# Value products of two heads in one 128-column matmul, with a new order of patterns and query loads

## The chip, the core and the metric

The kernel runs on one core of a Trainium2 chip. The metric is the device time of one execution in microseconds (us). The core has a matrix engine (PE, with its weight loads listed as PEld), a vector engine (DVE), a scalar engine (ACT), a general engine (POOL) and a queue (SP) that issues all DMA transfers of this kernel in the order of the program. Each engine runs its own instructions in program order and waits for the others through semaphores.

## What is computed

One layer of a hybrid decoder: 4096 prompt positions and 32 sample positions go through one input projection. Half of the result feeds attention with 8 heads of 64, half a gated recurrence; both are gated, joined, projected back and normalised. The part that the change touches is the prompt's attention. Each head looks back along the sequence in three patterns, (window, stride) = (128, 1), (512, 4) and (2048, 16), with 128 keys each:

```
def _dilated_prompt(q, k, v, d):
    """Dilation d: split positions into d stride classes (keys gathered by stride) and run
    the window attention inside each class."""
def _band_attention(q, k, v):
    s = jnp.einsum('nbqhd,nbkhd->nbhqk', qb, kc) * (dh ** -0.5)
    p = jnp.exp(s - m[..., None])
    o = jnp.einsum('nbhqk,nbkhd->nbqhd', p, vc) / den...
def _merge(parts):
    ws = [den * jnp.exp(m - m_max) for (_, m, den) in parts]
    return sum(w[..., None] * o for w, (o, _, _) in zip(ws, parts)) / total[..., None]
```

All values are float32.

## The kernel before, in words

Four phases follow one another. Phase 1 projects q, k and v. Phase 2 is the attention, with the matmuls of the attention's gate woven in as filler. Phase 3 is the recurrence, phase 4 the output projection, the normalisation and the sample's attention. The change lies in phase 2 (line 405), which takes the time from 592 to about 1490 us of the profiled execution.

Phase 2 works through 8 units. A unit is a pair of heads and one half of the sequence (2048 positions, in four spans of 512). The keys of the pair lie in the tile `KT` (`S1` or `S_77` in the traces), its queries in `QT` (`S0`, `S_76`), one quarter of which belongs to each span `nb`. A unit has 48 steps. A step is 128 queries of one pattern for both heads. In the code the pattern `pat` is 0 for stride 16, 1 for stride 4 and 2 for stride 1. The order of a unit's steps is written out in the list `order` (line 738): four steps of stride 4 and four of stride 1 on span 0, then 16 steps of stride 16 (`a` = 0 to 3, over all spans), then four of stride 4 and four of stride 1 on each of the spans 1 to 3. A span is complete with the fourth step (`b` = 3) of its last pattern; span 0 with the last step of stride 16.

Step `i` is spread over the loop of line 772, which counts steps in `now`:

- `gather_q` (line 457), three steps ahead: POOL copies the step's queries in stride order into `qg`. Stride 1 needs no gather; PE reads `QT` itself.
- `front` (line 510), at step `i`: PE writes the scores of both heads into `s` (lines 515 and 516, two matmuls a head), DVE adds the mask and takes the minimum (line 522), ACT takes the exponential (line 526) into `sm`.
- `feed`: about four filler matmuls (lines 653 to 658, 256 columns each).
- `middle` (line 529), two steps later: PE transposes `sm` into `pt` (line 535), DVE or ACT copies it to `pts` (lines 539 and 541); the list `ev` says which.
- `back` (line 543), four steps later: PE multiplies `pts` by the values into `o` (line 551).

In most steps the band has two blocks of 128 keys (`x.full`); at the start of the sequence it has one. I call them full and half steps. All patterns' first steps of a sequence are half steps: 21 of the 48 steps in the units with the first half of the sequence (units 0, 2, 4 and 7), none in the others. That is 300 full and 84 half steps.

`back` before the change: for each block of keys and each head one matmul with the 64 value columns of the head as stationary operand and 128 moving columns; head 0 writes partitions 0 to 63 of `o`, head 1 partitions 64 to 127. Four steps fill a bank of `o`; after the fourth, ACT copies the whole bank to `u` in SBUF.

Merging the three patterns runs along behind, by calls that `defer` puts a number of steps after the end of a span: `stats_out` (3 steps), `stats_in` (6), `weights` (11), `weights_b` (12), `spread` (15, the DMA `gb<-wd` that brings the weights back, spread over partitions), `combine` (17 to 20, five POOL instructions on the tile `gb`, the first in line 620, the others recorded in line 798) and `store` (21). `load_Q` (line 396, four DMAs of 256 KB) fetches the next unit's queries of a span two steps after the span's end. POOL runs gathers and combines in one order, SP runs all DMAs in one order.

Of the kernel before, what the change touches and what calls it, by code (L numbers as in the profile page):

```python
# [8 lines left out]
F32 = mybir.dt.float32  # L9
# [14 lines left out]
SPAN = 512  # L24
# [6 lines left out]
class Kern:  # L31
# [373 lines left out]
    def phase2(self):  # L405
# [136 lines left out]

        def back(x):
            kbs = (0, 1) if x.full else (1,)
            if x.b == 0:
                x.grp.o = ps_o.tile([128, 512], F32, tag="o", name="o")
            o = x.grp.o
            for kb in kbs:
                v = v_ap(x.c, x.st, x.pat, x.a, x.b, kb)
                for h in range(2):  # L550
                    nc.tensor.matmul(o[h * 64:(h + 1) * 64, x.b * 128:(x.b + 1) * 128],  # L551
                                     v[:, h * 64:(h + 1) * 64], x.pt[:, h, kb],
                                     start=(kb == kbs[0]), stop=(kb == 1), skip_group_check=True)
            if x.b == 3:
                if x.pat == 0:
                    nc.scalar.copy(x.unit.u16.rearrange("p (i r) -> p r i", r=16)[:, 4 * x.a:4 * x.a + 4],
                                   o.rearrange("p (r i) -> p r i", r=4))
                else:
                    t = up.tile([128, SPAN], F32, tag=f"u{x.pat}", name="u", bufs=4 - x.pat)
                    if x.pat == 1:  # L560
                        nc.scalar.copy(t.rearrange("p (m r) -> p r m", r=4), o.rearrange("p (r m) -> p r m", r=4))
                    else:
                        nc.scalar.copy(t, o)
                    x.unit.u[x.pat, x.a] = t


        def stats_out(un, nb):
# [43 lines left out]
        def combine(un, nb):  # L611
            s, gb = slice(nb * SPAN, (nb + 1) * SPAN), un.gb[nb]
            e = nc.gpsimd
            for k, (f, o, y) in enumerate(((e.tensor_mul, 0, un.u16[:, s]), (e.tensor_mul, 1, un.u[1, nb]),
                                           (e.tensor_mul, 2, un.u[2, nb]), (e.tensor_add, 0, gb[:, 1]),
                                           (e.tensor_add, 0, gb[:, 2]))):
                if k:
                    defer(min(k, 3), f, gb[:, o], gb[:, o], y)
                else:
                    f(gb[:, o], gb[:, o], y)  # L620
# [114 lines left out]
            units.append(un)  # L735
        steps = []
        for un in units:
            order = [(1, 0), (2, 0)] + [(0, w) for w in range(4)]
            for nb in range(1, 4):
                order += [(1, nb), (2, nb)]  # L740
            for pat, a in order:
                grp = S()
                for b in range(4):
                    x = S()
                    x.unit, x.c, x.st, x.pat, x.a, x.b, x.grp = un, un.c, un.st0, pat, a, b, grp
                    steps.append(x)
# [18 lines left out]

        vload(0)
        vload(4)
        for x in steps[:3]:
            gather_q(x)
        feed(self.f0[0])  # L770
        N, staged, split = len(steps), 0, 0
        for i in range(N + 26):
            now[0] = i
            if i < N:
                x = steps[i]
                un = x.unit
                if x.pat == 1 and x.a == 0 and x.b == 0:
                    un.u16 = u16p.tile([128, ST], F32, tag="u16", name="u16")
                    un.ac = sp.tile([128, 3, 16, 2, 2], F32, tag="ac", name="ac")
                    if un.i < 6 and un.st0 == 0:  # L780
                        defer(self.kl[0], load_K, un.c, 4, 2)
                        defer(self.kl[1], load_K, un.c, 6, 2)
                if x.pat and x.b == 0:
                    un.st[x.pat, x.a] = sp.tile([128, 4, 2, 2], F32, tag=f"st{x.pat}", name="st")
                x.stat = un.ac[:, 0, 4 * x.a + x.b] if x.pat == 0 else un.st[x.pat, x.a][:, x.b]
                front(x)
# [3 lines left out]
            if 0 <= i - 2 < N:  # L790
                middle(steps[i - 2])
            if i + 3 < N and steps[i + 3].pat < 2:
                gather_q(steps[i + 3])
            for k in (1, 5):
                if i + k < N and (steps[i + k].pat == 0) == (k == 1):
                    vload(i + k)
# [5 lines left out]
            if i >= self.wl[1] and credit[0] < -10 ** 8:  # L802
                for _ in range(self.wl[2]):
                    if split < staged:
                        wx_split(split)
                        split += 1
            if i < N and x.b == 3 and (x.pat == 2 and x.a or x.pat == 0 and x.a == 3):
                nb = x.a if x.pat else 0
                for d, f in zip(self.lag, (stats_out, stats_in, weights, weights_b, spread, combine)):
                    defer(d, f, un, nb)  # L810
# [1 line left out]
                if un.i + 1 < 8:  # L812
                    v = units[un.i + 1]
                    if nb == self.kl[4] and un.i % 2 and un.i < 6:
                        defer(self.kl[5], load_K, v.c, 0, 2)
                        defer(self.kl[6], load_K, v.c, 2, 2)
                    if nb and un.i == 5:
                        if nb < 3:
                            defer(self.kl[2], load_K, v.c, 3 + nb, 1)
                        else:  # L820
                            defer(self.kl[3], load_K, v.c, 6, 2)
                    defer(2, load_Q, v.c, v.st0, nb)
        assert split == 8
        while credit[0] > -10 ** 8 or later:
            now[0] += 1
# [789 lines left out]
def tile_hymba_dilated_attn_rglru(ctx, tc, ins, outs):  # L1615
# [3 lines left out]
    k.kl, k.lag, k.f0, k.wl, k.fill_rate = k.p2[:7], k.p2[7:13], k.p2[13:18], k.p2[18:20] + (2,), (k.p2[20],) * 8  # L1619
    k.t0x = 1.5, 1.5, (1,) * 8, (1, 1, 0, 1, 1, 0, 1, 1)  # L1620
    k.t0 = -9.0, 22.2, 23.0
    k.ev = 0, 1, 0, 0
    k.p4 = 6.55, 12.0, 13.5, 14.1, 18.2, 9.0, 2.0, 6.5
    k.ls = 356, 358, 360, 364, 366, 368, 370, 372, 374, 376
    k.nx = lambda nc, t, c: nc.gpsimd if t == 0 and c % 2 else None
# [42 lines left out]
```

## Time and profile before

| | us |
|---|---|
| median of 3 runs | 2416.06 (2415.0 to 2421.57) |
| the profiled execution, its own time | 2421.3 |
| its span, first to last instruction | 2419.3 |
| phase 2 in it, about | 592 to 1490 |
| PE busy over the span | 2247.5 (93%) |
| DVE, ACT, POOL busy over the span | 1476.3, 1028.6, 860.5 |
| mean granted TensorE clock | 0.97 of full speed |

A row of the trace names the line, the engine, the operation, the tile written and the tiles read, and how many instructions it stands for. Matmuls are pipelined: the time of one is longer than the distance to the next, so it is the distance between starts that counts. What an engine waited for stands in brackets behind the idle time before it.

### The profile page before, as it was taken

How to read it: one execution, taken by the hardware profiler on the slowest of the kernel's cores; microseconds unless marked ns; L12 is line 12 of the kernel's file. 1: busy time of each engine (PE TensorE's matmuls, PEld its weight loads, DVE VectorE, ACT ScalarE, POOL GpSimd, SP SyncE). 2: the span in 40 equal slices, each digit the busy share in tenths (PEclk: the TensorE clock that was granted, in tenths of full speed). 3: DMA queues.
4: the chain of work that ended last, by engine and by line, in shares of the span. 5: the costliest groups of instructions: out<-in, count | busy, mean ns of one | idle time of the engine just before them, and what ended most of it. 6: DMA issues, size and time to landing. Idle time of an engine off the chain costs nothing. (4 is left out here: it accounts for less than half of the span.)

```text
span 2419.3 us, 42698 instructions
## 1 busy us (share of the span) xinstructions
PE 2247.5 (93%) x15274; PEld 1890.9 (78%) x15274; DVE 1476.3 (61%) x3511; ACT 1028.6 (43%) x2691; POOL 860.5 (36%) x628
## 2 busy tenths in 40 slices
PE   6999999997999899979988988799999978989998
PEld 5878888886788778868777877799999956657776
DVE  4323222232576757646655655688999989998444
ACT  3212122222666566646655654455565632222221
POOL 1000000000445546464636465333333446656111
PEclk9999999998999999989999998899999999989999
DMA  6854556649676866777696755455545556668551
GB/s 173 257 189 153 174 174 200 209 186 245 181 171 169 203 158 174 181 181 172 161 203 173 172 143 137 154 171 153 162 157 176 193 176 226 239 223 324 204 187 57
DMA packets 324947, 444.18 MB, mean 184 GB/s; under 512 B 58629, under 2 KB 193413, under 8 KB 319617
## 3 DMA queue, kind: packets, MB, share of 16 engines
q1 hardware_dynamic: 324576, 440.94, 62.2%
q8 instruction: 122, 2.00, 0.4%
q14 instruction: 89, 0.72, 0.1%
q0 software_dynamic: 160, 0.52, 0.1%
HBM read 305.79 MB, written 135.60 MB: 182 GB/s over the span
## 5 line engine op out<-in xcount | busy, mean ns | idle before, releaser
L465 POOL CAST qg<-S 128x512 fp32r<-128x512 f32 x256 | 275.2, 1106 | 619.4 <-DMA S<-qd 482.6
L1280 PE MATMUL po<-S,mx 128*128 128x512 f32 x1536 | 377.5, 405 | 27.1 <-DVE xr L1334 17.1
L1280 PEld LDWEIGHTS po<-S,mx 128*128 128x128 f32 x1536 | 292.2, 192 | 118.3 <-issue 29.5
L522 DVE CUSTOM_DVE_ANT_0 sm<-s,mask 128x256 f32<-128x256 f32 (+1 forms) x768 | 270.8, 390 | 159.7 <-PE s L516 111.4
L526 ACT ACTIVATE sm<-sm,st 128x256 f32<-128x256 f32 (+1 forms) x512 | 251.7, 493 | 156.4 <-DVE st L522 130.4
L535 PE MATMUL pt<-ident,sm 128*128 128x128 f32 x1368 | 238.6, 292 | 11.1 <-ACT sm L526 10.9
L551 PE MATMUL o<-pts,v 128*64 128x128 f32 x2736 | 238.6, 290 | 7.6 <-DMA v<-vd 4.2
L539 DVE COPY pts<-pt 128x512 f32<-128x512 f32 x228 | 157.4, 690 | 138.5 <-PE pt L535 108.5
L515 PE MATMUL s<-S,qg 128*128 128x256 f32 x512 | 160.9, 334 | 54.2 <-POOL qg L465 53.1
L535 PEld LDWEIGHTS pt<-ident,sm 128*128 128x128 f32 x1368 | 144.9, 143 | 79.9 <-issue 55.5
L203 DVE TENSOR_TENSOR stg<-pp,stg 128x512 fp32r<-128x512 f32 x56 | 51.2, 917 | 238.7 <-ACT stg L202 234.1
L551 PEld LDWEIGHTS o<-pts,v 128*64 128x64 f32 x2736 | 143.9, 138 | 62.5 <-issue 3.6
L188 PE MATMUL pp<-S,xh 128*128 128x512 f32 x768 | 179.3, 394 | 6.4 <-ACT S L127 5.4
L314 PE MATMUL pp<-xh,S 128*128 128x512 f32 x448 | 176.0, 393 | 0.0
L188 PEld LDWEIGHTS pp<-S,xh 128*128 128x128 f32 x768 | 145.6, 190 | 38.5 <-ACT S L127 6.2
L315 PE MATMUL pp<-xh,S 128*128 128x512 f32 x448 | 174.5, 389 | 0.8 <-POOL xh L114 0.8
L316 PE MATMUL pp<-xh,S 128*128 128x512 f32 x448 | 174.6, 390 | 0.0
L526 ACT ACTIVATE sm<-sm,ac 128x128 f32<-128x128 f32 (+1 forms) x256 | 114.2, 447 | 109.5 <-DVE ac L522 109.2
L139 PE MATMUL xl<-xh,S 128*128 128x256 f32 x512 | 147.5, 288 | 8.9 <-DMA xh<-xtd 6.9
L143 PE MATMUL xl<-xh,S 128*128 128x256 f32 x512 | 147.7, 289 | 1.7 <-POOL S L128 1.3
L653 PE MATMUL f<-xh,S 128*128 128x256 f32 x512 | 147.3, 288 | 2.2 <-DMA xh<-xtd 2.1
L515 PEld LDWEIGHTS s<-S,qg 128*128 128x128 f32 x512 | 100.3, 196 | 62.5 <-POOL qg L465 59.9
(289 smaller groups left out, 5512.9 us busy)
## 6 DMA issues: line engine op xcount, KB each, us to landing
xh<-xtd SPq DMA_DIRECT2D x256, 256.0 KB, 5.4
S<-qd SPq DMA_DIRECT2D x128, 256.0 KB, 5.2
xtd<-xh SPq DMA_DIRECT2D x56, 512.0 KB, 2.6
gb<-wd SPq DMA_DIRECT2D x64, 384.0 KB, 6.2
v<-vd SPq DMA_DIRECT2D x264, 64.0 KB, 4.7
S<-kd SPq DMA_DIRECT2D x64, 256.0 KB, 7.2
xr<-in_x_prompt_dram SPq DMA_DIRECT2D x32, 512.0 KB, 4.8
arena<-in_cache_k_dram SPq DMA_DIRECT2D x16, 1024.0 KB, 9.0
```

What stands on the lines that cost most here:

```text
L188: nc.tensor.matmul(p, l, m, start=(c == 0 and a + b == 0), stop=(c == 7 and (a, b) == ((1, 0) if j < 2 else (0, 1))))
L314: nc.tensor.matmul(ps, wh, xh, start=(c == 0), stop=False)
L315: nc.tensor.matmul(ps, wh, xl, start=False, stop=False)
L316: nc.tensor.matmul(ps, wl, xh, start=False, stop=(c == 7))
L465: nc.gpsimd.tensor_copy(o, q.bitcast(F32))
L515: nc.tensor.matmul(s[:, h], q_ap(x, h, 0), k, start=True, stop=False)
L522: nc.vector.tensor_tensor_reduce(x.sm[:, h, o], s[:, h, i], self.mask[:, x.pat, o], -0.125, 3e38, ALU.add, ALU.min, x.stat[:, h, 0:1])
L526: nc.scalar.activation(x.sm[:, h, o], x.sm[:, h, o], AF.Exp, bias=x.stat[:, h, 0:1], scale=-1.0, accum_out=x.stat[:, h, 1:2])
L535: nc.tensor.transpose(p[:, h, kb], x.sm[:, h, kb * 128:(kb + 1) * 128], self.ident)
L539: e(x.pt, p)
L551: nc.tensor.matmul(o[h * 64:(h + 1) * 64, x.b * 128:(x.b + 1) * 128], v[:, h * 64:(h + 1) * 64], x.pt[:, h, kb], start=(kb == kbs[0]), sto ...
L1280: self.nc.tensor.matmul(ps[j], l, self.Wo[j][c][:, s], start=(c == 0 and s == 0 and l is mh), stop=(c == 7 and l is ml))
```

## The change

In `back`, one matmul takes all 128 value columns (both heads) as stationary operand and both heads' 256 columns of `pts` as moving operand. Its result has four blocks of 64 partitions by 128 columns, of which two are wanted: head 0's values with head 0's weights, and head 1's with head 1's. A bank of `o` now holds two steps. After every second step ACT copies head 0's half of the partitions and DVE head 1's, 64 partitions by 256 elements each. `u` of stride 4 has two buffers in place of three, `u` of stride 1 three in place of two. Within a span, stride 1 goes ahead of stride 4. `combine` begins with stride 4's product. `load_Q` is issued one step after the gather of a span's last step is written, which is two steps ahead of that step, where before it was two steps behind it. Three of eight copies to `pts` are ACT's, where it was one of four.

```
         def back(x):
             kbs = (0, 1) if x.full else (1,)
-            if x.b == 0:
-                x.grp.o = ps_o.tile([128, 512], F32, tag="o", name="o")
+            if x.b % 2 == 0:
+                x.grp.o = ps_o.tile([128, 2, 2, 128], F32, tag="o", name="o")
             o = x.grp.o
             for kb in kbs:
-                v = v_ap(x.c, x.st, x.pat, x.a, x.b, kb)
-                for h in range(2):
-                    nc.tensor.matmul(o[h * 64:(h + 1) * 64, x.b * 128:(x.b + 1) * 128],
-                                     v[:, h * 64:(h + 1) * 64], x.pt[:, h, kb],
-                                     start=(kb == kbs[0]), stop=(kb == 1), skip_group_check=True)
-            if x.b == 3:
...
+                nc.tensor.matmul(o[:, x.b % 2], v_ap(x.c, x.st, x.pat, x.a, x.b, kb), x.pt[:, :, kb],
+                                 start=(kb == kbs[0]), stop=(kb == 1), skip_group_check=True)
+            if x.b % 2 == 0:
+                return
...
+                if x.b == 1:
+                    x.unit.u[x.pat, x.a] = up.tile([128, SPAN], F32, tag=f"u{x.pat}", name="u", bufs=1 + x.pat)
...
+            for h, e in enumerate((nc.scalar.copy, nc.vector.tensor_copy)):
+                r = slice(h * 64, (h + 1) * 64)
+                e(t[r, x.b - 1:x.b + 1], o[r, :, h])
...
-            for k, (f, o, y) in enumerate(((e.tensor_mul, 0, un.u16[:, s]), (e.tensor_mul, 1, un.u[1, nb]),
+            for k, (f, o, y) in enumerate(((e.tensor_mul, 1, un.u[1, nb]), (e.tensor_mul, 0, un.u16[:, s]),
...
-            order = [(1, 0), (2, 0)] + [(0, w) for w in range(4)]
+            order = [(2, 0), (1, 0)] + [(0, w) for w in range(4)]
...
-                order += [(1, nb), (2, nb)]
+                order += [(2, nb), (1, nb)]
...
-                gather_q(steps[i + 3])
+                y = steps[i + 3]
+                gather_q(y)
+                if y.b == 3 and (y.pat == 1 and y.a or y.pat == 0 and y.a == 3) and y.unit.i < 7:
+                    v = units[y.unit.i + 1]
+                    defer(1, load_Q, v.c, v.st0, y.a if y.pat else 0)
...
-                    defer(2, load_Q, v.c, v.st0, nb)
...
-    k.ev = 0, 1, 0, 0
+    k.ev = 0, 1, 0, 0, 1, 0, 0, 1
```

Matrix engine PE, one full step in the middle of phase 2, before (`f` filler, `o` value products, `pt` transposes, `s` scores; each product into `o` is written once here and runs as two instructions, since its operands are float32):

```order
L653 MATMUL f<-xh,S_78 128x256
L656 MATMUL f<-xh,S_78 128x256
L658 MATMUL f<-xh,S_78 128x256
L551 MATMUL o<-pts,v_11163 64x128 x2
L551 MATMUL o<-pts,v_11423 64x128 x2
L535 MATMUL pt<-ident,sm 128x128 x4
L515 MATMUL s<-S_77,S_76 128x256
L516 MATMUL s<-S_77,S_76 128x256
```

and the same place now:

```order
L651 MATMUL f<-xh,S_78 128x256
L654 MATMUL f<-xh,S_78 128x256
L656 MATMUL f<-xh,S_78 128x256
L549 MATMUL o<-pts,v_11000 128x256
L549 MATMUL o<-pts,v_11252 128x256
L535 MATMUL pt<-ident,sm 128x128 x4
L515 MATMUL s<-S_77,qg 128x256
L516 MATMUL s<-S_77,qg 128x256
```

The order of the stages on PE is the same; four products of 64 by 128 became two of 128 by 256.

POOL, the end of unit 0 and the start of unit 1, before (`qg` a gather of queries, `gb` the combine's five instructions):

```order
L798 TENSOR_TENSOR gb_5254<-gb_5254,u_4405 128x512
L798 TENSOR_TENSOR gb_5254<-gb_5254,u_4519 128x512
L798 TENSOR_TENSOR gb_5254<-gb_5254 128x512 x2
L465 CAST qg_5490<-S0_76 128x512
L465 CAST qg_5519<-S0_76 128x512
L465 CAST qg_5551<-S0_76 128x512
L465 CAST qg_5588<-S0_76 128x512
L620 TENSOR_TENSOR gb_5521<-gb_5521,u16_4146 128x512
L798 TENSOR_TENSOR gb_5521<-gb_5521,u_5047 128x512
L798 TENSOR_TENSOR gb_5521<-gb_5521,u_5155 128x512
L798 TENSOR_TENSOR gb_5521<-gb_5521 128x512 x2
```

and now:

```order
L465 CAST qg_5340<-S0_76 128x512
L798 TENSOR_TENSOR gb_5241<-gb_5241,u16_4140 128x512
L465 CAST qg_5367<-S0_76 128x512
L798 TENSOR_TENSOR gb_5241<-gb_5241,u_4356 128x512
L465 CAST qg_5401<-S0_76 128x512
L798 TENSOR_TENSOR gb_5241<-gb_5241 128x512 x2
L465 CAST qg_5441<-S0_76 128x512
L618 TENSOR_TENSOR gb_5500<-gb_5500,u_5087 128x512
L465 CAST qg_5590<-S0_76 128x512
L798 TENSOR_TENSOR gb_5500<-gb_5500,u16_4140 128x512
L465 CAST qg_5619<-S0_76 128x512
L798 TENSOR_TENSOR gb_5500<-gb_5500,u_4992 128x512
```

The four gathers of a span's stride-4 steps stood between two combines and stand inside them now, each behind an instruction of the combine.

SP, the DMAs at the end of unit 4, before (`S0` is the tile of queries, `gb<-wd` the weights that the combine waits for):

```order
L576 DMA ac_10118<-s4d_69 32x64
L576 DMA ac_10118<-s1d_70 32x64
L607 DMA gb_11520<-wd_71 64x3x512 x2
L445 DMA v1_11552<-vd_64 128x1x128 x4
L399 DMA S0_76<-qd_62 64x2x512 x4
L568 DMA s4d_69<-st_11301 128x16
L570 DMA s1d_70<-st_11436 128x4x4
```

and now:

```order
L574 DMA ac_9970<-s4d_69 32x64
L574 DMA ac_9970<-s1d_70 32x64
L399 DMA S0_76<-qd_62 64x2x512 x4
L605 DMA gb_11349<-wd_71 64x3x512 x2
L437 DMA v4_11377<-vd_64 32x4x128 x4
L566 DMA s4d_69<-st_11265 128x16
L568 DMA s1d_70<-st_11134 128x4x4
```

The load of the queries stood behind the pair of weight DMAs and stands directly ahead of it now.

## Rows read from the trace of the kernel before

**Rows 1.** The page: value products and query gathers (operation, count, busy us, mean ns, idle before)

```profile
L551 PE MATMUL o<-pts,v 128*64 128x128 f32 x2736 | 238.6, 290 | 7.6 <-DMA v<-vd 4.2 <-ACT u L563 2.3 <-DVE pts L541 0.8
L465 POOL CAST qg<-S 128x512 fp32r<-128x512 f32 x256 | 275.2, 1106 | 619.4 <-DMA S<-qd 482.6 <-PE s L516 103.3 <-PE f L658 14.2
```

**Rows 2.** Busy time by stretch, units 1, 2, 6: PE, PEld, DVE, ACT, POOL, clock, DMA

```profile
697.80:803.90 106.10, 99.73 (x916) 82.87 (x914) 69.89 (x256) 69.84 (x225) 56.82 (x50) 0.99 0.75 185
803.90:916.20 112.30, 102.93 (x883) 86.39 (x882) 74.78 (x295) 64.69 (x226) 61.11 (x55) 0.97 0.72 176
...
1252.00:1369.10 117.10, 106.61 (x962) 89.67 (x960) 70.74 (x256) 71.11 (x228) 61.70 (x55) 0.97 0.73 176
```

**Rows 3.** Timeline of PE, a full step of unit 2 (start us, us, operation)

```profile
900.07 0.28 PE L658 MATMUL f<-xh,S 128*128 128x256 f32 x1
900.28 0.66 PE L551 MATMUL o<-pts,v 128*64 128x128 f32 x8
900.87 0.66 PE L535 MATMUL pt<-ident,sm 128*128 128x128 f32 x4
901.28 0.37 PE L515 MATMUL s<-S,qg 128*128 128x256 f32 x1
...
902.20 0.28 PE L653 MATMUL f<-xh,S 128*128 128x256 f32 x1
902.42 0.66 PE L551 MATMUL o<-pts,v 128*64 128x128 f32 x8
```

**Rows 4.** Timeline of PE, a half step of unit 2

```profile
848.81 0.44 PE L551 MATMUL o<-pts,v 128*64 128x128 f32 x4
849.18 0.44 PE L535 MATMUL pt<-ident,sm 128*128 128x128 f32 x2
849.37 0.37 PE L515 MATMUL s<-S,qg 128*128 128x256 f32 x1
...
850.50 0.44 PE L551 MATMUL o<-pts,v 128*64 128x128 f32 x4
```

**Rows 5.** Timeline of PE, a half step of unit 0 that has no value product yet

```profile
604.22 0.28 PE L658 MATMUL f<-xh,S 128*128 128x256 f32 x1
604.34 0.38 PE L535 MATMUL pt<-ident,sm 128*128 128x128 f32 x2
604.47 0.36 PE L515 MATMUL s<-S,qg 128*128 128x256 f32 x1
```

**Rows 6.** Timeline of PE in phase 4: float32 products in four column groups, 512 moving columns

```profile
2156.50 1.90 PE L1486 MATMUL do<-arena,Z 128*8 128x512 f32 x16
2158.33 11.51 PE L1280 MATMUL po<-S,mx 128*128 128x512 f32 x48
```

**Rows 7.** Timeline of POOL, the end of unit 5 and the start of unit 6

```profile
1244.31 1.27 POOL L620 TENSOR_TENSOR gb<-gb,u 128x512 f32<-128x512 f32 x1 [25.65 <-DMA v<-vd]
1245.54 2.51 POOL L798 TENSOR_TENSOR gb<-gb,u 128x512 f32<-128x512 f32 x2
...
1250.57 4.35 POOL L465 CAST qg<-S 128x512 fp32r<-128x512 f32 x4
...
1276.14 4.05 POOL L465 CAST qg<-S 128x512 fp32r<-128x512 f32 x4 [7.60 <-DMA s4d<-st]
```

**Rows 8.** Timeline of SP's queue there: weights for the combine, then the query load

```profile
1254.39 1.23 SPq L607 DMA_DIRECT2D gb<-wd  x2
...
1264.93 2.55 SPq L399 DMA_DIRECT2D S<-qd  x4
```

**Rows 9.** Timeline of PE there: the score that waited for the gather

```profile
1277.23 0.58 PE L515 MATMUL s<-S,qg 128*128 128x256 f32 x1 [5.88 <-POOL qg L465]
```

**Rows 10.** Waits of all engines, 697 to 1480 us: total us, times, longest

```profile
ACT u L563 <- POOL gb L798: 73.1, 17, 6.6
...
PE s L515 <- POOL qg L465: 38.6, 22, 5.9
```

**Rows 11.** Instructions by line: a copy of 256 elements from PSUM, DVE

```profile
L541 DVE COPY pts<-pt 128x256 f32<-128x256 f32 x60 | 25.4, 424 | 43.2 <-PE pt L535 43.2
```

More of the change, by code (lines that the diff above doesn't have):

```diff
@@ L544, in back @@
             kbs = (0, 1) if x.full else (1,)
-            if x.b == 0:
-                x.grp.o = ps_o.tile([128, 512], F32, tag="o", name="o")
+            if x.b % 2 == 0:
+                x.grp.o = ps_o.tile([128, 2, 2, 128], F32, tag="o", name="o")
             o = x.grp.o
             for kb in kbs:
-                v = v_ap(x.c, x.st, x.pat, x.a, x.b, kb)
-                for h in range(2):
-                    nc.tensor.matmul(o[h * 64:(h + 1) * 64, x.b * 128:(x.b + 1) * 128],
-                                     v[:, h * 64:(h + 1) * 64], x.pt[:, h, kb],
-                                     start=(kb == kbs[0]), stop=(kb == 1), skip_group_check=True)
-            if x.b == 3:
[L555 to L564, printed above, removed]
+                nc.tensor.matmul(o[:, x.b % 2], v_ap(x.c, x.st, x.pat, x.a, x.b, kb), x.pt[:, :, kb],
+                                 start=(kb == kbs[0]), stop=(kb == 1), skip_group_check=True)
+            if x.b % 2 == 0:
+                return
+            if x.pat == 0:
+                t = x.unit.u16.rearrange("p (i r) -> p r i", r=16)[:, 4 * x.a:4 * x.a + 4]
+            else:
+                if x.b == 1:
+                    x.unit.u[x.pat, x.a] = up.tile([128, SPAN], F32, tag=f"u{x.pat}", name="u", bufs=1 + x.pat)
+                t = x.unit.u[x.pat, x.a]
+                t = t.rearrange("p (m r) -> p r m", r=4) if x.pat == 1 else t.rearrange("p (r m) -> p r m", r=4)
+            for h, e in enumerate((nc.scalar.copy, nc.vector.tensor_copy)):
+                r = slice(h * 64, (h + 1) * 64)
+                e(t[r, x.b - 1:x.b + 1], o[r, :, h])
         def stats_out(un, nb):
@@ L767, in phase2 @@
         vload(4)
-        for x in steps[:3]:
-            gather_q(x)
         feed(self.f0[0])
@@ L776, in phase2 @@
                 un = x.unit
-                if x.pat == 1 and x.a == 0 and x.b == 0:
+                if x.pat == 2 and x.a == 0 and x.b == 0:
                     un.u16 = u16p.tile([128, ST], F32, tag="u16", name="u16")
@@ L806, in phase2 @@
                         split += 1
-            if i < N and x.b == 3 and (x.pat == 2 and x.a or x.pat == 0 and x.a == 3):
+            if i < N and x.b == 3 and (x.pat == 1 and x.a or x.pat == 0 and x.a == 3):
                 nb = x.a if x.pat else 0
```

## The prediction

> **What bounds the kernel now.** I read the busy times by stretch first, cut at the starts of the units. In phase 2 PE is busy in 99.73 of 106.10 us of a unit of full steps; DVE, ACT and POOL are at 70, 70 and 57 [rows 2]. Then the timeline of PE, to see whether that is real work. A full step runs from one group of value products to the next, 900.28 to 902.42, 2.14 us, and nothing in it waits [rows 3]; a half step takes 1.69 [rows 4]. So PE sets the pace, and a nanosecond added to PE's step counts unless it falls where PE waits anyway. How much waiting is there? 48 full steps of 2.13 are 102.2 us; unit 1 took 106.1, unit 6 took 117.1. A unit with 27 full and 21 half steps would need 93; unit 2 took 112.3 [rows 2]. The surplus is 4 to 19 us a unit. The waits name its main source: PE waits 38.6 us in 22 places for POOL's gather [rows 10], and each of these pauses may be followed by a stretch at the lower of the clock's two levels, 1.2 in place of 2.4 GHz (the clock column is 0.97 in units 2 and 6 and 0.99 in unit 1) [rows 2].
>
> **Part 1: the value products on PE.** This is the large term, so I take it apart by distances between starts. The 8 instructions of a full step hold PE from 900.28 to 900.87, 0.59 us [rows 3]; the 4 of a half step from 848.81 to 849.18, 0.37 [rows 4]. Four more cost 0.22. That is two rounds of 0.11 for 128 moving columns, both heads at once: were the four run one after another, each would have to stream 128 columns in 0.055 us, while a float32 transpose of 128 columns takes 0.11 as well (0.41 for four in rows 3, 0.19 for two in rows 4). What is left of the half step's block is 0.37 - 0.22 = 0.15 that doesn't grow with the work. Two more such pieces stand around it: from the start of the last filler to the first product 0.21 [rows 3], where a filler takes 0.12 (604.22 to 604.34 in rows 5), so 0.09; and the transposes behind the products take 0.19 for two [rows 4], but 0.13 where no product stands ahead of them [rows 5], so 0.06. Together 0.30 us a step come with entering and leaving the products. Transposes right behind a filler show no such cost [rows 5]; they use the whole width of the array, the products half of it for each head.
>
> The Trainium skill says on the page "TensorEngine Tiling (Array Packing)", section Key Properties, that changing the tiling mode drains TensorE; the 0.30 us agree with that. The same page, When to Use Tiling, holds column tiling to be worth a factor of 2 for a stationary operand of 64 columns or less, and by that rule alone this change gives up half of PE's rate in these products.
>
> After the change both are gone: no switch, and no second head alongside. What does one instruction with 128 stationary and 256 moving columns in float32 cost? No row shows this shape. The nearest ones: rounds of 512 float32 columns, 16 instructions in four column groups, so four rounds, from 2156.50 to 2158.33; less 0.09 for leaving, 0.435 a round, or 0.217 for 256 columns [rows 6]. The rounds of 128 in 0.11 give 0.22 [rows 3, 4]. Fillers of 256 columns in the reduced float32 format take 0.12 [rows 5]; that is the lower bound, and it would hold if the rate of full float32 were a matter of the column groups. I take 0.217: three shapes with one, two and four groups agree on 0.85 ns a column, so groups don't set it.
>
> Full step: minus 0.59, 0.09 and 0.06, plus 4 x 0.217 = 0.87: +0.13 us. Half step: minus 0.37, 0.09 and 0.06, plus 0.43: -0.09. The 2736 instructions before [rows 1] are 8 in each of 300 full and 4 in each of 84 half steps, so **+39 and -7 us**. Most half steps belong to stride 16, where POOL has a gather (1.1 us) in each and a combine besides, and a shorter step only meets POOL sooner; I count half of the 7. **PE: +35.** At 0.22 an instruction it is +39.
>
> **Part 2: copies out of the bank.** Before, ACT made one copy of 512 elements a group; now ACT and DVE make two of 256 each on 64 partitions. DVE's copy of 256 elements out of PSUM takes 0.42 [rows 11]; 24 a unit are 10 us, less six copies to `pts` handed to ACT. DVE goes from 70 to about 76 of 108 us: hidden beside PE, 0. Uncovered, in a step that waits for DVE, it would cost its 0.42; a strided target might double that.
>
> **Part 3: query loads and order.** Four steps earlier means 8.5 us. The gathers at 1276.14 waited 7.60 us after POOL had finished its combine [rows 7], the load of these queries having been issued at 1264.93 [rows 8], and PE waited 5.88 for them [rows 9]. That wait goes; what is late next there is the combine, which ended about 1268.5 and would cost nothing. The pause also leaves the low clock behind. For this place and two weaker ones of its kind (units 2 and 4): **-9** (0 to -15). At the start of phase 2 the first score no longer waits for a gather: **-1.1** [rows 1]. In the full units a gather and a combine instruction for each of four steps, and two in the last, ask POOL for 4 x 1.09 + 1.27 + 2.51 + 2.63 = 10.8 us [rows 7], in four steps of 8.5 us before and 9.0 now: eight such places, half a microsecond each, and some pauses of PE that the longer step absorbs: **-8** (0 to -20).
>
> Against this stand two costs, seen in the order of the program. Gathers for stride 4 now stand inside the combine. Before, a gather behind a combine had eight steps, 17 us, until PE needed it, and 6.3 of combine plus 1.1 of itself ahead of it [rows 7], so a combine could start 9.6 us late; now it has four steps, 9.0 us, less 1.3 and 1.1: 6.6 us. A combine waits for the DMA of its weights (25.65 us in one row of rows 7, a wait whose harmless part I can't separate). And the megabyte of queries now stands ahead of these weights on SP, 2.55 us of issuing [rows 8]. SP waits there until POOL has made the span's last gather, and behind SP wait the weights that POOL waits for. Fifteen combines meet these gathers. At 3 us each the bound is +45, at none 0; I take a few of them, **+8**. The tile `u` of stride 4 has lost a buffer, and both copying engines wait where it is late; ACT's waits for `u` were 73.1 us in 17 places [rows 10] and mostly hidden, as this one should be: 0 to +10, within the range.
>
> **Sum:** 35 - 9 - 1 - 8 + 8 = +25 us on the profiled execution's 2421.3. That execution is 5 us above the median of the runs, so on the median's footing 2416 + 25 = 2441; I round to **2440 us**.
>
> **Rivals.** *The pauses go (faster).* If the earlier loads and the longer step take away the surplus at the unit ends and in the stride-16 blocks, PE's floor decides: four units of 48 x 2.26 = 108.5 us, where unit 1 took 106.1 and unit 6 117.1, and three of 27 x 2.26 + 21 x 1.60 = 94.6, where unit 2 took 112.3. It begins to be faster when 35 us of pauses vanish. With unit 6's surplus gone in two units (2 x 14) and two thirds of unit 2's in one and a half (18), plus the 8 above, it is -54 + 35: about 2397 to 2405. For it: the 38.6 us of waiting on gathers [rows 10]. Against: rows 7 show the combine, not the queries, as the first thing late at 1244, and the combine now stands nearer to PE.
> *The combine binds.* Every late combine costs 3 us and a stretch of low clock: +20 more, 2460.
> *Nothing is seen.* The pauses absorb the added PE time one for one: 2416.
> *The products run at 0.12.* Then PE's step falls by 0.25 us in full steps, 75 us in all, until POOL and ACT bind; about 2360.
> *The 0.30 us stay.* If they come from the step between float32 products and what stands around them rather than from the two column groups, all of 384 x 0.30 = 115 us comes on top: 2555. Rows 5 speak against it.
>
> **How the numbers follow.** Forecast 0.50, combine 0.13, the 0.30 stay 0.03 (slower together 0.66); nothing seen 0.13 (same); pauses go 0.16, products at 0.12 0.05 (faster 0.21). A change below 0.3% (7 us) can't be told from none here. The likeliest case alone spans 2425 to 2455. The range reaches from the pauses' case to the late combines, 2400 to 2470.
>
> **What would show it.** In the trace after: four products at distances of 0.217 us and no gap ahead of the transposes (right), or 0.12 (the lower bound). A full step of 2.26 us where nothing waits. No wait for queries behind the last combine at a unit's end. PE's waits for POOL's gathers at the fourth step ahead of a unit's end show the combine's price. The sum is wrong if the pauses change by more than 20 us, since PE's term is known to a few.

## The result and the profile after

The changed kernel takes **2588.23 us** (median of 4 runs, 2585.04 to 2590.95) against 2418.82 us for the kernel before in the same session (2415.0 to 2423.94). The ratio is **1.070, interval 1.067 to 1.073**: 169 us slower. The forecast was 2440, with a range up to 2470. The direction was right and the size was not.

The page of the changed kernel, its head and three groups (operation, count, busy us, mean ns, idle time before it and what ended it). Line 549 is now the value product, 562 the copies into `u`, 618 the first instruction of the combine.

```profile
span 2584.0 us, 40248 instructions
...
PE 2318.9 (90%) x13906; PEld 2008.9 (78%) x13906; DVE 1541.7 (60%) x3655; ACT 1051.7 (41%) x2835; POOL 858.2 (33%) x628
...
L549 PE MATMUL o<-pts,v 128*128 128x256 f32 x1368 | 390.8, 405 | 132.7 <-DVE pts L539 111.9
...
L562 DVE COPY u<-o 64x256 f32<-64x256 f32 x192 | 106.1, 553 | 413.6 <-ACT u L562 413.5
```

The product's idle time grew from 7.6 us [rows 1] to 132.7, and what ended it is DVE's copy of the transposes. DVE's own new copy stood idle for 413.5 us because of ACT's. Before, the product waited 0.8 us for a copy by DVE [rows 1], and DVE made no copy of `u`.

Busy time by stretch, units 1, 2 and 6, columns as in [rows 2].

```profile
712.40:845.50 133.10, 110.83 (x725) 98.83 (x722) 78.23 (x273) 72.96 (x241) 58.75 (x52) 0.95 0.67 152
845.50:980.50 135.00, 110.96 (x734) 99.29 (x732) 79.68 (x316) 67.33 (x246) 58.34 (x52) 0.95 0.60 143
1382.80:1517.50 134.70, 116.19 (x769) 105.24 (x767) 78.10 (x275) 72.83 (x242) 58.71 (x52) 0.94 0.61 149
```

A unit went from 106.1, 112.3 and 117.1 us [rows 2] to 133.1, 135.0 and 134.7. PE's idle part of unit 1 went from 6 to 22 us, and the clock fell from 0.99 to 0.95. The page's 165 us of longer span are all in phase 2: from its first score to its last it took 882 us before (592.3 to 1474.4) and takes 1052 now (590.3 to 1641.9). Over the whole span PE is busy 71 us longer (2247.5 to 2318.9) and idle 93 us longer. The steps' own price (+0.13 us on 300 full and -0.09 on 84 half steps, 31 us) is less than half of the busy part; the granted clock, 0.958 where it was 0.970, is part of the rest.

The timeline of PE, a full step and a half step where nothing waits; they answer to [rows 3] and [rows 4].

```profile
1080.64 1.03 PE L549 MATMUL o<-pts,v 128*128 128x256 f32 x4
1081.51 0.60 PE L535 MATMUL pt<-ident,sm 128*128 128x128 f32 x4
1081.86 0.37 PE L515 MATMUL s<-S,qg 128*128 128x256 f32 x1
...
1082.90 1.03 PE L549 MATMUL o<-pts,v 128*128 128x256 f32 x4
```

```profile
918.67 0.28 PE L654 MATMUL f<-xh,S 128*128 128x256 f32 x1
918.78 0.59 PE L549 MATMUL o<-pts,v 128*128 128x256 f32 x2
919.21 0.38 PE L535 MATMUL pt<-ident,sm 128*128 128x128 f32 x2
919.35 0.36 PE L515 MATMUL s<-S,S 128*128 128x256 f32 x1
...
920.38 0.59 PE L549 MATMUL o<-pts,v 128*128 128x256 f32 x2
```

This is the step that was forecast: four products in 0.87 us (1080.64 to 1081.51), so 0.217 each; a full step of 2.26; a half step of 1.60 (918.78 to 920.38); products 0.11 behind the filler, and transposes of 0.14 for two, with nothing left of the 0.30 us around the products. The loss is in steps that wait. One of them, step 43 of unit 3, on the timeline of all engines (only the rows of the chain):

```profile
1085.93 3.60 SPq L399 DMA_DIRECT2D S<-qd  x4
...
1091.11 1.82 SPq L605 DMA_DIRECT2D gb<-wd  x2
...
1100.16 1.26 POOL L618 TENSOR_TENSOR gb<-gb,u 128x512 f32<-128x512 f32 x1 [35.63 <-DMA gb<-wd]
1101.37 1.08 POOL L465 CAST qg<-S 128x512 fp32r<-128x512 f32 x1
1101.45 0.60 ACT L562 COPY u<-o 64x256 f32<-64x256 f32 x1 [11.59 <-POOL gb L618]
1102.09 0.61 DVE L562 COPY u<-o 64x256 f32<-64x256 f32 x1 [13.24 <-ACT u L562]
...
1102.73 0.69 DVE L539 COPY pts<-pt 128x512 f32<-128x512 f32 x1
...
1103.48 1.36 PEld L549 LDWEIGHTS o<-pts,v 128*128 128x128 f32 x4 [11.73 <-DVE pts L539]
1103.48 2.08 PE L549 MATMUL o<-pts,v 128*128 128x256 f32 x4 [11.53 <-DVE pts L539]
```

Read it downwards. The query load is issued ahead of the weights `gb<-wd`; the combine on POOL waits for these weights; ACT's copy waits for the combine, because both buffers of stride 4's `u` are full; DVE's copy waits for ACT's copy of the other half of the same bank into the same `u`; the transposes that PE needs stand behind it on DVE; PE waits 11.53 us. Then PE runs at about the lower of its two clock levels, 1.2 GHz: the four products take 2.08 in place of 1.03, and the granted clock of the stretch behind the pause is 0.54 (busy times by stretch):

```profile
1103.40:1110.00 6.60, 6.52 (x25) 5.68 (x26) 4.65 (x15) 3.45 (x11) 6.52 (x7) 0.54 0.04 11
```

The waits of all engines from 590 to 1645 us (total us, times, longest) tell how often:

```profile
DVE u L562 <- ACT u L562: 405.7, 187, 14.1
POOL gb L618 <- DMA gb<-wd: 238.9, 13, 35.6
...
PE o L549 <- DVE pts L539: 107.1, 44, 11.5
ACT u L562 <- POOL gb L618: 102.6, 22, 11.6
...
PE s L515 <- POOL qg L465: 18.9, 16, 3.6
```

The chain also feeds itself: SP waits 131.7 us for weights that DVE has yet to make (`wd<-wg`, line 597, from 590 to 1650 us), where it waited 38.4 before, so a held DVE can make the next combine later. No run takes this link out by itself.

Four links of one chain are candidates: the query loads, the gathers and the combine on POOL, the buffers of `u`, and DVE behind ACT. A chain in a trace doesn't tell which link is worth what; the runs do.

### The profile page after: what moved, and what is told of

Read it like the earlier page. It is cut to its first block, busy times and chain, and to the rows that moved or that the text cites. A ratio compares the mean times of both kernels' runs of the same rounds, so it can differ in the third digit from the quotient of the medians.

```text
span 2584.0 us, 40248 instructions
## 1 busy us (share of the span) xinstructions
PE 2318.9 (90%) x13906; PEld 2008.9 (78%) x13906; DVE 1541.7 (60%) x3655; ACT 1051.7 (41%) x2835; POOL 858.2 (33%) x628
## 5 line engine op out<-in xcount | busy, mean ns | idle before, releaser
L549 PE MATMUL o<-pts,v 128*128 128x256 f32 x1368 | 390.8, 405 | 132.7 <-DVE pts L539 111.9
L549 PEld LDWEIGHTS o<-pts,v 128*128 128x128 f32 x1368 | 243.9, 200 | 170.5 <-DVE pts L539 124.5
L562 DVE COPY u<-o 64x256 f32<-64x256 f32 x192 | 106.1, 553 | 413.6 <-ACT u L562 413.5
L535 PE MATMUL pt<-ident,sm 128*128 128x128 f32 x1368 | 221.6, 281 | 0.0
L535 PEld LDWEIGHTS pt<-ident,sm 128*128 128x128 f32 x1368 | 180.9, 146 | 43.1 <-issue 4.3
L515 PE MATMUL s<-S,qg 128*128 128x256 f32 x512 | 163.0, 338 | 34.1 <-POOL qg L465 18.9
L618 POOL TENSOR_TENSOR gb<-gb,u 128x512 f32<-128x512 f32 x32 | 40.6, 1269 | 428.4 <-DMA gb<-wd 251.1
L139 PE MATMUL xl<-xh,S 128*128 128x256 f32 x512 | 146.3, 286 | 7.0 <-DMA xh<-xtd 7.0
L651 PE MATMUL f<-xh,S 128*128 128x256 f32 x512 | 147.4, 288 | 1.4 <-DMA xh<-xtd 1.4
L654 PE MATMUL f<-xh,S 128*128 128x256 f32 x512 | 146.9, 287 | 0.0
```

The lines of the kernel that those rows point to most:

```text
L515: nc.tensor.matmul(s[:, h], q_ap(x, h, 0), k, start=True, stop=False)
L535: nc.tensor.transpose(p[:, h, kb], x.sm[:, h, kb * 128:(kb + 1) * 128], self.ident)
L549: nc.tensor.matmul(o[:, x.b % 2], v_ap(x.c, x.st, x.pat, x.a, x.b, kb), x.pt[:, :, kb], start=(kb == kbs[0]), stop=(kb == 1), skip_group_c ...
L651: nc.tensor.matmul(o, wh, xt[c][:, 0], start=(c == 0 and m == 0), stop=False, skip_group_check=True)
```

## The experiments

Three theories went in. A: stride 4's two buffers hold ACT, and DVE behind it. B: DVE's copy behind ACT's copy of the same tile costs by itself. C: query loads and order make the combine late and put it in the gathers' way. Differences with a sign below are against the kernel before on the same chip. Where two other kernels are compared, their times are taken as they stand; the kernel before itself took 2418.82 to 2424.18 us in these sessions, so such a difference is good to some 5 us.

### One part of the change at a time

**Products only.** Products, bank and two copies stay; step order, query loads and combine order go back to those of before. `u` has three buffers of both kinds, and `w` and `wg` pay for the space with one each. Against the changed kernel:

```diff
-            order = [(2, 0), (1, 0)] + [(0, w) for w in range(4)]
+            order = [(1, 0), (2, 0)] + [(0, w) for w in range(4)]
...
-  u[x.pat, x.a] = up.tile(..., bufs=1 + x.pat)
+  u[x.pat, x.a] = up.tile(..., bufs=3)
```

> The new products, bank layout and two-half copies alone, in the step order, with the query loads and the combine order of the kernel before; both `u` tiles get three buffers (the two small weight tiles w and wg of the combine give up one buffer each for the space). Theory A (the waits come from stride 4's `u` having two buffers, taken two steps earlier than before, so that ACT waits for POOL's combine and DVE waits behind ACT): nothing of that can happen here, so what is left is the products' own price, +0.13 us on 300 full and -0.09 us on 84 half steps of PE, and the time is 2420 to 2460 us. Theory B (DVE's copy behind ACT's copy of the same tile costs by itself, at every second step, whatever the buffers): 2530 to 2590 us, with `DVE u <- ACT u` still above 250 us. Theory C (the query loads and the step order make the combine late): as under A, since neither is in this kernel; 2420 to 2460 us.

Measured: 2496.59 us, ratio 1.030 (1.027 to 1.033), +73 us, between the theories. No wait of ACT for POOL's combine is among its longer waits, yet DVE waits behind ACT (590 to 1650 us):

```profile
DVE u L562 <- ACT u L562: 303.5, 190, 7.3
...
PEld o L549 <- DVE pts L539: 34.3, 58, 1.5
```

Its timeline shows a usual place:

```profile
1180.61 0.35 ACT L562 COPY u<-o 64x256 f32<-64x256 f32 x1
...
1180.99 0.43 DVE L562 COPY u<-o 64x256 f32<-64x256 f32 x1 [1.32 <-ACT u L562]
...
1181.45 0.69 DVE L539 COPY pts<-pt 128x512 f32<-128x512 f32 x1
...
1182.19 1.13 PE L549 MATMUL o<-pts,v 128*128 128x256 f32 x4 [0.31 <-DVE pts L539]
```

ACT reaches its copy behind two exponentials; DVE idles 1.32 us until ACT has finished, and PE is late by 0.31. A quarter of the distances from one step's scores to the next's is 2.62 us or more here, where the middle one is 2.26.

**Order only.** The products, the single copy and ACT's one of four copies to `pts` of before, in the new order with its early query loads. Against the changed kernel:

```diff
-                nc.tensor.matmul(o[:, x.b % 2], v_ap(...), x.pt[:, :, kb], ...)
+                for h in range(2):
+                    nc.tensor.matmul(o[h * 64:(h + 1) * 64, ...], v[:, h * 64:(h + 1) * 64], x.pt[:, h, kb], ...)
...
-    k.ev = 0, 1, 0, 0, 1, 0, 0, 1
+    k.ev = 0, 1, 0, 0
```

> The step order, combine order and early query loads of the changed kernel, with the products and the one copy of four steps of the kernel before; stride 4's `u` has two buffers but is taken only at the group's fourth step, two steps later than in the changed kernel, and DVE copies none of it. Theory A: ACT's wait for POOL shrinks to less than 40 us and holds nothing of DVE; 2405 to 2450 us. Theory B: as A, 2405 to 2450 us. Theory C (early query loads ahead of the weights on SP's queue make the combines late and PE waits for gathers behind them): 2500 us or more.

Measured: 2501.96 us, ratio 1.032 (1.029 to 1.035), +79 us, and DVE has no copy of `u` here at all. Theory C holds. PE's waits for gathers are up:

```profile
PE s L515 <- POOL qg L465: 112.5, 39, 11.0
```

The kernel before has 53.1 us in 23 places in the same stretch, and 14.5 of them are the first score of phase 2, whose wait of 12.2 us is here one for the query load.

**The third buffer.** The changed kernel whole, with three buffers for stride 4 as well.

```diff
-  u[x.pat, x.a] = up.tile(..., bufs=1 + x.pat)
+  u[x.pat, x.a] = up.tile(..., bufs=3)
```

> The changed kernel with three buffers for stride 4's `u` as well (the small weight tiles w and wg of the combine have one buffer in place of two, for the space). Theory A: ACT's wait for POOL (102.6 us) goes, with it most of DVE's 405.7 us behind ACT and PE's 107 us for pts; 2440 to 2480 us. Theory B: DVE still waits behind ACT at every second step; 2550 to 2600 us. Theory C: the combine is as late as it was, and holds gathers; 2540 to 2600 us.

Measured: 2536.01 us, ratio 1.046 (1.042 to 1.050): 52 us less than the changed kernel, above the range of theory A and below those of B and C. ACT no longer waits for the combine, and PE's waits for `pts` fall from 107.1 to below 15 us, but others take their place (590 to 1650 us):

```profile
DVE u L562 <- ACT u L562: 300.7, 190, 7.1
...
PE s L515 <- POOL qg L465: 91.9, 38, 9.0
```

So the changed kernel's 18.9 us of waits for gathers were no gain of the earlier query loads; PE was stopped earlier in the same steps, by another wait.

**Both halves by ACT.** The changed kernel, with its two buffers; DVE copies nothing out of the bank.

```diff
-            for h, e in enumerate((nc.scalar.copy, nc.vector.tensor_copy)):
+            for h, e in enumerate((nc.scalar.copy, nc.scalar.copy)):
```

> The changed kernel with both halves of a bank copied by ACT, two buffers for stride 4 as in the changed kernel. Theory A: ACT is held by POOL as before and, with it, its three of eight copies of the transposed probabilities and its exponentials; DVE is free; 2560 to 2620 us. Theory B: the wait of DVE behind ACT is gone; 2430 to 2500 us. Theory C: 2560 to 2600 us, as for the changed kernel.

Measured: 2512.04 us, ratio 1.037 (1.034 to 1.040): 76 us less, in none of the ranges (12 us above that of B), while ACT waits for POOL even longer than in the changed kernel:

```profile
ACT u L562 <- POOL gb L618: 137.6, 23, 12.8
```

A held ACT is borne much better than a held DVE. No single theory is enough after these four.

### Which link is worth what

**Order only, query loads late.** As "order only", with the query loads two steps after the span's last step, where they were before.

```diff
-                if y.b == 3 and ...: defer(1, load_Q, v.c, v.st0, ...)
...
+                    defer(2, load_Q, v.c, v.st0, nb)
```

> As e2_order_only (the step order alone, 2502 us), but with the query loads where the kernel before has them, two steps after the span's last step, behind nothing new on SP. Theory C1 (the early query loads hold the weights on SP's queue and so the combine): the time falls by 40 us or more, to 2420 to 2460 us, and POOL's wait for the weights falls from 212 us towards the 100 us of the kernel before. Theory C2 (the combine is no later than it was, but in the new order the four gathers of the next stride-4 group stand behind it on POOL, where in the old order they stood ahead of it): no gain, 2490 to 2520 us, and PE's waits for gathers stay above 90 us.

Measured: 2446.64 us, ratio 1.009 (1.007 to 1.012). 55 of the 79 us are gone with nothing but the loads moved. SP's queue and POOL at the same place of unit 3's end tell why. First "order only", then this kernel:

```profile
1067.01 3.31 SPq L399 DMA_DIRECT2D S<-qd  x4
1070.42 1.23 SPq L607 DMA_DIRECT2D gb<-wd  x2
```

```profile
1079.26 1.26 POOL L620 TENSOR_TENSOR gb<-gb,u 128x512 f32<-128x512 f32 x1 [12.59 <-DMA gb<-wd]
```

```profile
1040.37 1.25 SPq L607 DMA_DIRECT2D gb<-wd  x2
1041.72 1.96 SPq L437 DMA_DIRECT2D v<-vd  x4
1043.79 3.66 SPq L399 DMA_DIRECT2D S<-qd  x4
```

```profile
1047.01 1.28 POOL L620 TENSOR_TENSOR gb<-gb,u 128x512 f32<-128x512 f32 x1 [9.86 <-DMA gb<-wd]
```

With the queries ahead, the weights are issued 3.4 us later (1067.01 to 1070.42), and the combine starts 8.84 us after that; with the queries behind, 6.64 us (1040.37 to 1047.01). Here the combine is 5.6 us later for it. The traces show the same wherever a load stands ahead, which is in two combines of each of the units 0 to 6: on average these 14 start 9.5 us after the issue of their weights in "order only" and 7.3 us with late loads. The other 14 of these units have no load ahead in either kernel and start after 7.7 us in both. Counted from the first score of their span's last step, the first 14 start at 50.7 us with early loads and at 43.9 with late ones, which is also the figure of the kernel before.

**Order only, gathers ahead of the combine.** Query loads early, but the four gathers of a stride-4 group are written at the first step of the stride-1 group ahead of it, so that they stand ahead of the combine on POOL.

```diff
-                gather_q(y)
+                if y.pat == 0:
+                    gather_q(y)
...
+            if i + 4 < N and steps[i + 4].pat == 1 and steps[i + 4].b == 0:
+                for k in range(4, 8):
+                    gather_q(steps[i + k])
```

> As e2_order_only (2502 us), with the early query loads kept, but the four gathers of a stride-4 group are all written at the first step of the stride-1 group ahead of it, and so stand ahead of the combine on POOL; no further buffer is needed, since stride-1 steps use none. Theory C1: no gain, 2480 to 2510 us. Theory C2: the pauses of steps 43 and 3 (78 us over the units in e2_order_only) go, PE's waits for gathers fall below 50 us; 2415 to 2450 us.

Measured: 2457.97 us, ratio 1.014 (1.012 to 1.017), 44 us less, 8 above the range of C2. PE's waits for gathers fell as expected (590 to 1650 us):

```profile
PE s L515 <- POOL qg L465: 45.4, 23, 4.3
```

The combine is nearly as late as it was (49.8 us by the count above), but it no longer holds what PE needs.

**Both repairs of the order.** Query loads late and gathers ahead.

> The step order alone with both repairs: query loads two steps after the span's last step (as e5, +22 us against the kernel before) and the four gathers of a stride-4 group written ahead of the combine (as e6, +34 us). If what e5 has left over is the gathers behind the combine (21.8 us of excess at step 43), this is within 8 us of the kernel before, 2411 to 2427 us. If the order has a price of another kind (transfers of queries and values in another sequence), it stays at 2435 to 2450 us.

Measured: 2419.18 us, ratio 0.999 (0.998 to 1.000). The new order costs nothing by itself; its 79 us are a combine that is late, and gathers that stand inside and behind it.

**Products only, both halves by ACT.** As "products only", with DVE taken out of the copies.

```diff
-            for h, e in enumerate((nc.scalar.copy, nc.vector.tensor_copy)):
+            for h, e in enumerate((nc.scalar.copy, nc.scalar.copy)):
```

> As e1_products_only (products, bank layout and two-half copies in the old order with three buffers, 2497 us), but ACT copies both halves and DVE none. Theory P (all of the 74 us there is the products' own price on PE and the half clock that follows): no change, 2490 to 2500 us. Theory B (about half of it is DVE standing behind ACT's copy of the same tile, 303 us of waits in 190 places): 2445 to 2470 us, which leaves the products' price of some 35 us.

Measured: 2441.20 us, ratio 1.008 (1.006 to 1.010). 55 of the 73 us go with DVE's copies, although ACT now makes 384 copies in place of 192. The remaining +17 hold the products, the new bank, ACT's additional copies and the single buffers of `w` and `wg` together.

**The changed kernel with late query loads.**

> The changed kernel whole, with only its query loads put back to two steps after the span's last step. If the three causes seen so far add up (query loads ahead of the weights on SP about 55 us, DVE standing behind ACT's copy of the same tile about 55 us, the two buffers of stride 4's `u` about 52 us, the products about 20 us), the first alone is gone: 2525 to 2545 us. If the query loads only matter where the buffers are enough, or the buffers only matter because of the query loads, the gain differs: 2490 us or less (the combine then comes in time, and the buffers' wait goes with it), or 2570 us or more.

Measured: 2527.98 us, ratio 1.046 (1.044 to 1.047): 60 us less than the changed kernel. ACT's wait for the combine also fell, from 102.6 to 52.2 us (590 to 1650 us).

**All three removed.** Three buffers, ACT for both halves, late query loads; products, bank, step order and combine order of the changed kernel.

> The changed kernel with the three suspected causes taken away together: three buffers for stride 4's `u` (one for w and wg), both halves of a bank copied by ACT, query loads two steps after the span's last step. The products, the bank layout, the step order and the combine order stay. If these three are all of it, what stays is the products' price and the gathers behind the combine: 2435 to 2465 us. If a fourth cause is left, above 2480 us.

Measured: 2457.55 us, ratio 1.016 (1.014 to 1.018), +38 us: 131 of the 169 us are gone. What is left agrees with the sum of two others: +17 for the products (ACT copies, old order) and +22 for the order with late query loads.

**The same with the old products.** Two matmuls of 64 columns in place of one of 128, into the same places of the bank.

```diff
-                nc.tensor.matmul(o[:, x.b % 2], v_ap(...), x.pt[:, :, kb], ...)
+                for h in range(2):
+                    nc.tensor.matmul(o[h * 64:(h + 1) * 64, x.b % 2, h], v[:, h * 64:(h + 1) * 64], x.pt[:, h, kb], ...)
```

> As f2_all_three, but each product in two matmuls of 64 columns as in the kernel before, written into the same places of the new bank; the same copies follow. By the rows of PE (full step 2.26 us with the new products against 2.13 us, half step 1.60 against 1.69 us) the new products cost some 35 us: this kernel then is 15 to 40 us faster than f2_all_three. If the products' price is hidden by other waits, the two are within 8 us.

Measured: 2448.63 us, ratio 1.012 (1.010 to 1.014). The new products are 9 us dearer, less than expected, and the four runs of this kernel themselves lie 9 us apart. PE is busy 17.6 us less in this kernel (2261.6 against 2279.2); pauses take up about half of that.

**One engine a bank.** As "all three removed", but DVE copies both halves of a group's first bank and ACT both of its second.

```diff
-            for h, e in enumerate((nc.scalar.copy, nc.scalar.copy)):
+            for h, e in enumerate(((nc.vector.tensor_copy, nc.scalar.copy)[x.b // 2],) * 2):
```

> As f2_all_three (2458 us), but ACT copies both halves of a group's second bank only, and DVE both halves of its first. Both engines write the same `u` as in the changed kernel, but DVE now writes it two steps ahead of ACT and waits for no copy of the same moment; ACT has to wait for DVE's copies, which lie two steps back. If the damage came from DVE standing behind ACT in the same step: 2445 to 2465 us, with no wait of DVE for ACT's copy and less than 20 us of waits of ACT for DVE's. If sharing a tile between the two engines costs whatever the moment: 2490 us or more.

Measured: 2459.36 us, ratio 1.016 (1.014 to 1.018), the same as with ACT alone, and no wait of DVE for ACT's copy is left in its list. So two engines may write one `u`, and DVE may make half of the copies. What costs is that one of them has to wait for the other's copy of the same moment. Whether it waits for the sake of the shared `u` or of the shared bank of `o` is not settled: two copies of one moment share both in the changed kernel and neither here.

### A way to halve the switch

If the 0.30 us around the products come from going to the half-array form and back, they can be paid once for two steps. Both kernels are the one before, with the products of two steps written together, the first with a fourth buffer for the copied transposes.

```diff
-            if 0 <= i - 4 < N:
-                back(steps[i - 4])
+            if 0 <= i - 4 < N and i % 2:
+                back(steps[i - 5])
+                back(steps[i - 4])
```

> The kernel before, with its 64-column products and its order, but the products of two steps written one behind the other at every second step (four buffers for the copied transposes, one for w and wg): if the 0.30 us around the products of a full step is the price of going to the half-array form and back, it is paid half as often, 0.15 us on some 384 steps: 58 us less on PE, and 2360 to 2400 us. If the pauses and the clock take most of it back, 2400 to 2420 us; if pairing starves PE of other work, above 2430 us.

Measured: 2410.96 us, ratio 0.995 (0.993 to 0.996).

The second takes the pair one step earlier, so that three buffers do for the transposes and stride 1's `u` gets a third:

```diff
+            if 0 <= i - 3 < N and i % 2 == 0:
+                back(steps[i - 4])
+                back(steps[i - 3])
...
+  t = up.tile(..., bufs=3)
```

> As c1_paired_products (2411 us), but the pair is taken one step earlier, so that three buffers do for the transposes, and the space goes to a third buffer of stride 1's `u`, for which ACT waits 96 us there. If that wait is what eats c1's gain: 2375 to 2400 us. If the odd step's products come too soon behind their transposes: PE waits for pts, and 2410 to 2440 us.

Measured: 2406.26 us, ratio 0.995 (0.993 to 0.997), the lowest time here, though by its ratio no faster than the first, and 6 us above what I had expected of it. Its timeline of PE shows the pair:

```profile
1189.82 1.09 PE L551 MATMUL o<-pts,v 128*64 128x128 f32 x16
1190.85 0.66 PE L535 MATMUL pt<-ident,sm 128*128 128x128 f32 x4
...
1192.30 0.60 PE L535 MATMUL pt<-ident,sm 128*128 128x128 f32 x4
...
1193.79 1.09 PE L551 MATMUL o<-pts,v 128*64 128x128 f32 x16
```

Two steps take 3.97 us in place of 4.26, and 16 products 1.03 (1189.82 to 1190.85) where 8 took 0.59 [rows 3]: the fixed part is paid once. PE is busy 2203.2 us, 44 less than before, but the time fell by 13. The rest went into waits: PE's for the gathers are 71.3 us, against 53.1 before, and those of the products for `pts` 17.6, against 0.8.

## Why the prediction was wrong, point by point

**Right: PE's own step.** All numbers of Part 1 came out within 0.01 us: 0.217 for a product, 2.26 and 1.60 for the steps, the 0.30 us gone. The two rivals about this price (0.12 a product, the 0.30 us stay) are out. The Trainium skill (TensorEngine Tiling (Array Packing), Key Properties) has a change of tiling mode drain TensorE; the paired kernels agree, since two steps' products together pay the fixed part once. The +35 us of the sum were too many: where nothing else was in the way, the whole set of products, bank and copies by ACT cost 17, and the products' form alone 9. So the forecast direction came out by luck: it rested on this term (without it the sum is -10), and the term is at most a tenth of the 169 us.

**Wrong: "hidden beside PE, 0" (Part 2).** I priced DVE's copy by its busy time and compared that with DVE's free share. Busy time was nearly right (106 us in 192 copies, 553 ns each, 424 in [rows 11]). The step that failed was not asking what DVE's copy waits for, and what stands behind it. It waits for ACT's copy of the same bank into the same `u`, which stands behind ACT's exponentials; behind it on DVE stand the transposes' copies that PE needs next. Measured: 55 us ("products only" with and without DVE's copies), and nothing where DVE copies without that wait ("one engine a bank"). The Trainium skill (Perfetto Trace Analysis, Tensor Engine Instruction (MATMUL, LD_WEIGHTS)) calls ACT, DVE and GpSimd strict FIFO; the rows at 1102.09 and 1102.73 agree, since the copy to `pts` came out only behind the copy that had waited 13.24 us.

**Wrong: the buffer of `u`, "0 to +10, mostly hidden" (Part 3).** ACT's 73.1 us of waits before [rows 10] were hidden, as far as the runs tell, because nothing urgent stood behind them on DVE: the second paired kernel has rid itself of 96 us of them and has the ratio of the first, 0.995. In the changed kernel they hold DVE as well. Measured: 52 us (third buffer). I reasoned from how well the old wait was hidden, and the change took away the reason that it was. This term and the one above are one chain and don't add: with late query loads, taking both away gave 70 us (2527.98 to 2457.55).

**Wrong in sign: the query loads, -9 us.** The waits that I counted did go: the first score of phase 2 starts at 590.3 in place of 592.3, and no score at unit 6's start waits for queries as in [rows 9]. But PE still waits 5.70 us in step 3 of unit 6 (up to 1396.43), now for `pts` and through the chain above, and the loads now stand ahead of the combine's weights on SP. The text had this, with 2.55 us of issuing [rows 8], and gave it part of a +8; the other wait that it named, of SP for the span's last gather, is 3.9 us in all. Measured: +60 in the changed kernel, +55 in the order alone. What was left out is the transfer: the weights are not only issued 3.4 us later, they also take 2.2 us longer behind a megabyte, on average over 14 combines as in the one shown.

**Mis-sized: late combines in the gathers' way, +8 (0 to +45).** The mechanism is right; in the order alone steps 43 and 3 of the units take 78 us more in all than the usual 2.13 or 1.7 us, which is over the bound. At step 43 of units 1, 3 and 5 it is over 10 us each, where the bound took 3 us for every combine. By the count above, the 14 combines with a load ahead start 6.8 us later than before in the order alone, and 10.9 in the changed kernel. With late query loads 22 us stay, and they vanish when the gathers stand ahead.

**The account of the 169 us**, by the runs and with the causes taken away in this order: 60 query loads, 70 buffers and DVE behind ACT together, 39 left, of which some 17 belong to the products and some 22 to the gathers behind the combine. Of the -8 for absorbed pauses no run tells anything by itself; PE's idle time over the span grew from 172 to 265 us.

Of the rivals, "the combine binds" named the place and gave it 20 us. "The pauses go" fell with the sign of the query loads.

## What to carry to other kernels

Price a new instruction by what it waits for and what stands behind it on its engine, not by its busy time; splitting one copy between two engines made a wait between them in 187 of 192 copies here, and none once each engine had banks of its own. A wait that is hidden today is no measure of the same wait once another engine hangs on it. Before a load is moved earlier, look at the small transfers behind it in the queue: here 1 MB of queries, issued four steps earlier, cost 60 us through 0.75 MB of weights.

## What the runs showed of the hardware that was not expected

- The weights' read takes longer behind a large load: from its issue to the combine's start 8.84 us with four query loads of 256 KB directly ahead of it on SP, 6.64 us with them behind, and on average 9.5 against 7.3 us over 14 combines each.
- A copy on 64 partitions is no cheaper than one on 128: DVE took 0.43 us for each of the 64 copies of 64x256 from the bank to consecutive elements, against 0.424 for 128x256 [rows 11].
- A strided target costs: the other 128 copies of 64x256, for strides 4 and 16, took 0.59 to 0.65 us, which makes the mean of 0.553. In the kernel before, ACT's copy of 128x512 took 0.578 us to consecutive elements and 1.086 and 1.038 for the other two patterns.
- Pairs of half-array products go at 0.44 us for eight more (1.03 less 0.59); the other 0.15 of a group's 0.59 are a fixed price for each entry.
